# A second sum of squares in SBUF instead of PSUM, and two thirds of the rate for the third pair's input

## The chip, the core and the metric

The kernel runs on one core of a Trainium2 chip. The metric is the device time of one execution, in microseconds. The core has a matrix engine (PE, with its weight load PEld), a vector engine (DVE), a scalar engine (ACT), GpSimd (POOL) and SyncE (SP), which in this kernel issues every DMA in one queue. Matmuls write to PSUM, which the kernel divides into eight banks; everything else is kept in SBUF.

## The reference

One layer of a hybrid encoder: a mixer (retention heads and a convolution module, a joint projection `w_out`) and an MLP, each between two RMSNorms.

```python
mix = jnp.concatenate([ret_out, conv_out.astype(x.dtype)], axis=-1) @ w_out
x = x + rms_norm(mix, g_post_mix)          # first sum of squares: of mix
h = rms_norm(x, g_pre_mlp)                 # second sum of squares: of the new x
f = jnp.square(jax.nn.relu(h @ w_mlp_in)) @ w_mlp_out
x = x + rms_norm(f, g_post_mlp)
```

`d_model` is 1024, the MLP is 4096 wide, and there are 2048 prompt frames, 16 meta tokens and 8 streams of 16 frames. `rms_norm` divides by the root of the mean square over the 1024 channels. All is in fp32; each fp32 product is made of three matmuls of a high and a low part.

## The kernel before, in words

Channels lie on partitions (8 tiles of 128), tokens in the free dimension. The tokens are cut into six blocks (`gi` 0 to 5) of 256 or 384 columns. First the mixer runs over all blocks and leaves the output of `w_out` in DRAM (`yscr`). Then the MLP runs over three pairs of blocks, `G` = 0, 1, 2 (blocks 1 and 2, 3 and 4, 5 and 0), in halves of 384, 384 and 320 columns. For each pair it goes through sixteen blocks `b` of the hidden width. Each `b` has seven products of the first layer (`product`, lines L1207 to L1209, 12 matmuls each; a two by two Strassen scheme), between which lies the second layer of the block before. In `G` = 0, and at the ends of the other pairs, that is plain tiles (`l2_tile`, L514 to L516 through `mm3`, added by L1313). In `G` = 1 and 2, from `b` = 3 to 14, it is fourteen products of a second Strassen scheme (`l2_product`, L1295 to L1297, added to `ya` in SBUF by DVE at L1300). So such a `b` has 21 steps and, after each, a `tick()`.

Weights of the first layer come as prepared products `wp` from DRAM (L296, through SP); those of the second are loaded raw (L338) and prepared on ACT and POOL (L355, L356). Both take turns in one pool of nine buffers, so SP often waits until PE has used one up. L1242 makes differences of three tiles in SBUF on DVE, L383 and L384 split an operand in high and low on ACT and POOL.

Beside the MLP of a pair runs the preparation of the next pair's input: `prologue(G + 1)`, put in the queue "mlp" after `b` = 2. It is a generator; `tick()` advances it by one step when `ticks[0] % slow[0] == 0`, with `slow[0] = 2`. At `b` = 15 `drain("mlp")` would run what is left, and `reload` (L653) then brings the result back to SBUF. The steps are, for each of the two blocks, `mlp_in`:

- first pass: load `yscr` (L549), square on ACT (L501, L504), sum on DVE (L506, L509);
- the sum is copied to SBUF (L571), summed over partitions by a matmul with ones (L473), and eight DVE operations make the reciprocal root in the same PSUM bank, `sw` (L452 to L462), which is read as `rs`;
- second pass: load `yscr` and `x`, scale by `rs` on DVE (L582), add `x` on POOL (L584), store `x1d` (L585), square, and sum again (L506, L509);
- the same copy, matmul and reciprocal root; third pass: load `x1d`, scale (L590), store `hd` (L592).

That is 8 steps in each pass and 2 behind each of the two sums, 28 for a block. Then come `differences` (L614 to L623: loads of `hd`, sixteen subtractions on POOL, stores to `td`), 20 steps, so 76 in all.

The three PSUM pools are `mmp` (3 banks, first layer), `cvp` (2 banks, `l2y` and `mmc`) and `auxp` (3 banks). `auxp` holds `l2w` and `mma` of the second layer, and also the preparation's sum of squares `pacc` and its `sw`. The pool `np_` in SBUF holds `acc` (2 buffers) and `s` (5 buffers). The order of instructions on each engine is not the program's alone: a planner orders them by priority and by its own model of their times, and gives out free buffers as it goes; the preparation has a lower priority (`later["mlp"] = 100`).

Of the kernel before, what the change touches and what calls it, by code (L numbers as in the profile page):

```python
# [12 lines left out]
F32 = mybir.dt.float32  # L13
F32R = mybir.dt.float32r
I32 = mybir.dt.int32
AF = mybir.ActivationFunctionType
# [4 lines left out]
P = 128  # L21
D_MODEL, SEQ, N_META, PAST_LEN = 1024, 2048, 16, 512
# [147 lines left out]
def build(nc, T):  # L170
    lg = _log_gamma()
    with tile.TileContext(nc, schedule_with_timeline_sim=True) as tc, ExitStack() as top:
# [8 lines left out]
        np_ = ep(tc.tile_pool(name="np_", bufs=2))  # L181
# [13 lines left out]
        def pcol(n, i):  # L195
            return par[:, PC[n] + i:PC[n] + i + 1]
# [215 lines left out]

        heads_done = {}

        ticks, slow = [0], [1]

        def tick_heads():
# [29 lines left out]
        def rsqrt(ss, n, y, t, y1, z, r):  # L447


            f = 0.703952253  # L450
            w = 0.375 * f
            nc.vector.tensor_scalar(out=y.bitcast(I32), in0=ss.bitcast(I32), scalar1=-0.5,  # L452
                                    scalar2=float(0x5F1FFFF9) + math.log2(n) * 2.0 ** 22, op0=ALU.mult, op1=ALU.add)
            nc.vector.tensor_tensor(out=t, in0=y, in1=y, op=ALU.mult)
            nc.vector.scalar_tensor_tensor(out=t, in0=t, scalar=-1.0 / n, in1=ss, op0=ALU.mult, op1=ALU.mult)
            nc.vector.scalar_tensor_tensor(out=y1, in0=t, scalar=2.38924456, in1=y, op0=ALU.add, op1=ALU.mult)
            nc.vector.tensor_tensor(out=z, in0=y1, in1=y1, op=ALU.mult)
            nc.vector.scalar_tensor_tensor(out=z, in0=z, scalar=f * f * w ** 0.5 / n, in1=ss, op0=ALU.mult,
                                           op1=ALU.mult)
            nc.vector.scalar_tensor_tensor(out=z, in0=z, scalar=-10.0 / 3.0 * w ** 0.5, in1=z, op0=ALU.add,  # L460
                                           op1=ALU.mult)
            nc.vector.scalar_tensor_tensor(out=r, in0=z, scalar=5.0 * w, in1=y1, op0=ALU.add, op1=ALU.mult)  # L462
            return r
# [4 lines left out]
        def rstd_wide(acc, W, n, out=None):  # L468

            ps = auxp.tile([P, 512], F32, tag="aux", name="sw")[:, :W]  # L470
            accs = acc if isinstance(acc, list) else [acc]
            for i, a in enumerate(accs):
                nc.tensor.matmul(ps, ones, a, start=(i == 0), stop=(i == len(accs) - 1))  # L473
            yield WAIT
            yt = st_tile()
            y, t = yt[:, :W], yt[:, NM:NM + W]
            return rsqrt(ps, n, y, t, y, t, ps if out is None else out)

        def rstd_bcast(acc, W, n):

            starts = list(range(0, W - P + 1, P))
            if starts[-1] + P < W:
                starts.append(W - P)
            nb = len(starts)
            ps = auxp.tile([P, 4, P], F32, tag="aux", name="st")
            for b, s in enumerate(starts):
                nc.tensor.matmul(ps[:, b, :1], acc[:, s:s + P], ones[:, :1], start=True, stop=True)
            y = rsqrt_small(ps[:, :nb, 0], nb, n)
            dg = spool.tile([P, NM // P, P], F32, tag="dg", name="dg", bufs=1)
            for b in range(nb):  # L490
                nc.vector.tensor_scalar(out=dg[:, b, :], in0=ident, scalar1=y[:, b:b + 1], scalar2=None, op0=ALU.mult)
            yield WAIT
            rb = auxp.tile([P, 512], F32, tag="aux", name="rb")
            for b, s in enumerate(starts):
                nc.tensor.matmul(rb[:, s:s + P], ones, dg[:, b, :], start=True, stop=True)
            return rb[:, :W]
# [22 lines left out]
        WM = max(g["W"] for g in LAY)  # L519
# [10 lines left out]
        def st_tile():  # L530
            return stqs[0].tile([P, 2 * NM], F32, tag="st", name="st")

        def s_tile(N):
            return np_.tile([P, WM], F32, tag="s", name="s", bufs=SB)[:, :N]

        def mlp_in(gi):

            g = LAY[gi]
            N, W, m = g["N"], g["W"], g["meta"]
            G, off = PAIR[gi]  # L540
            early = G == 0

            def loads(src, two):

                ahead = []
                for k in range(KT + 1):
                    if k < KT:
                        y = s_tile(N)
                        nc.sync.dma_start(y, src(k))  # L549
                        xk = None  # L550
                        if two:
                            o = g["off"] * KT + k * W + m
                            xk = s_tile(N)
                            nc.sync.dma_start(xk, T["x"][:, o:o + N])
                        ahead.append((k, y, xk))
                    if k:
                        yield ahead.pop(0)

            def summed():
                if early:  # L560
                    return np_.tile([P, WM], F32, tag="acc", name="acc")[:, :N]
                return auxp.tile([P, 512], F32, tag="aux", name="pacc")[:, :N]

            def norm(acc):
                if early:
                    rb = yield from rstd_bcast(acc, N, D_MODEL)
                    rs = tp.tile([P, WM], F32, tag="rs", name="rs", bufs=1)[:, :N]
                    nc.scalar.activation(out=rs, in_=rb, func=AF.Copy)
                    return rs
                sb = np_.tile([P, WM], F32, tag="acc", name="acc")[:, :N]  # L570
                nc.scalar.activation(out=sb, in_=acc, func=AF.Copy)  # L571
                yield WAIT
                return (yield from rstd_wide(sb, N, D_MODEL))

            acc = summed()
            for k, y, _ in loads(lambda k: yscr[gi][k], False):
                add_square(acc, y, k, N)
                yield
            rs = yield from norm(acc)
            acc = summed()  # L580
            for k, y, xk in loads(lambda k: yscr[gi][k], True):
                nc.vector.scalar_tensor_tensor(out=y, in0=y, scalar=pcol("g_post_mix", k), in1=rs, op0=ALU.mult,  # L582
                                               op1=ALU.mult)
                nc.gpsimd.tensor_tensor(out=y, in0=y, in1=xk, op=ALU.add)  # L584
                nc.sync.dma_start(x1d[G][k][:, off:off + N], y)  # L585
                add_square(acc, y, k, N)
                yield
            rs = yield from norm(acc)
            for k, y, _ in loads(lambda k: x1d[G][k][:, off:off + N], False):
                nc.vector.scalar_tensor_tensor(out=y, in0=y, scalar=pcol("g_pre_mlp", k), in1=rs, op0=ALU.mult,  # L590
                                               op1=ALU.mult)
                nc.sync.dma_start(hd[G][k][:, off:off + N], y)  # L592
                yield
# [775 lines left out]
        for G, b, steps in plan():  # L1369
            if b == 0:  # L1370
                drain("norm")
                ya = {(c, r): x1p.tile([P, 4, NM], F32, tag=f"ya{c}{r}", name=f"ya{c}{r}")
                      for c in range(2) for r in range(2)}
            rate["norm"] = 2
            if b == NFB - 1:
                drain("mlp")
            cur, run = layer1(G, b)
            w, ybanks = {}, {}
            for what, x in steps:
                if what == "p":  # L1380
                    next(run)
                    tick()
                elif what == "w":
                    w[x] = next_unit("l2", G, x)
                elif what == "q":
                    wq = next_unit("q", G, x)
                elif what == "u":
                    l2_product(G, b - 1, *x, wq, prev, ya, ybanks)
                    tick()
                else:  # L1390
                    q, o, c = x
                    l2_tile(G, b - 1, c, q, o, w[b - 1, q], prev, ya)
                    tick()
            if b == 2 and G + 1 < NG:
                slow[0] = 2
                queues["mlp"].append(prologue(G + 1))
            if b == NFB - 1:
                if G + 1 < NG:
                    end_layer2(G, b, [w[b, q] for q in range(FB)], cur, ya)
                else:  # L1400
                    last_layer2(G, [w[e, q] for e in (b - 1, b) for q in range(FB)], (prev, cur), ya)
            prev = cur
# [59 lines left out]
```

## Time and profile before

| what | before |
|---|---|
| median of 3 runs | 2396.88 us (2394.41 to 2402.88) |
| the profiled execution | 2391.47 us |
| its span, first to last instruction | 2389.3 us |
| mean granted clock of PE | 0.992 |
| PE busy | 2302.5 us, 96% |
| DVE, POOL, ACT busy | 71%, 63%, 42% |

The mixer takes about the first 945 us of the span. `G` = 0 follows until about 1450, `G` = 1 until about 1950, `G` = 2 until the end. Times of the trace are in us from the start of the span. "Idle before" is the time in which an engine stood still ahead of an instruction, with what released it. A busy PE is not PE at its peak, since its matmuls overlap; where a pace matters, the count of matmuls in a stretch is the better measure.

### The profile page before, as it was taken

To read this page: it belongs to the slowest core of one execution; us is meant where nothing else is said; L and a number is where in the kernel's file an instruction comes from. 1 tells how busy PE (TensorE), PEld (TensorE's weight loads), DVE (VectorE), ACT (ScalarE), POOL (GpSimd) and SP (SyncE) were. 2 spreads that over 40 slices of the span, in tenths; PEclk is the share of its full clock that TensorE was granted. 3 is DMA by queue.
4 is the path that set the end of the run, shared out by engine and by line. 5 is a ranking of instruction groups with operands and counts; after the bars stand their busy time and mean duration, and the time that the engine had idled before them with its cause. 6 is when DMAs were issued, how large, how long until landed. Compare 5 with 4: busy or idle time off the path is not lost. (4 is left out here: it accounts for less than half of the span.)

```text
span 2389.3 us, 41429 instructions
## 1 busy us (share of the span) xinstructions
PE 2302.5 (96%) x14250; PEld 2267.5 (95%) x14250; DVE 1697.1 (71%) x3658; ACT 1002.7 (42%) x2240; POOL 1498.5 (63%) x1562
## 2 busy tenths in 40 slices
PE   8898999999999998999999999999999999999997
PEld 7898999999999998999999999998899999999996
DVE  8999997798988963356643357688776676566666
ACT  5534434124233234444444455344444443544442
POOL 7846232132234136878797775687897747888874
PEclk9999999999999999999999999999999999999998
DMA  8787788898789878568796557666764567555562
GB/s 315 279 314 265 270 294 287 219 336 314 236 292 339 288 268 316 205 215 300 265 329 210 187 203 253 227 222 217 260 220 160 185 221 253 187 193 181 193 218 89
DMA packets 248993, 586.90 MB, mean 246 GB/s; under 512 B 32080, under 2 KB 110160, under 8 KB 248784
## 3 DMA queue, kind: packets, MB, share of 16 engines
q1 hardware_dynamic: 248784, 584.28, 71.9%
q8 instruction: 112, 1.84, 0.3%
q14 instruction: 97, 0.79, 0.1%
HBM read 444.42 MB, written 139.75 MB: 244 GB/s over the span
## 5 line engine op out<-in xcount | busy, mean ns | idle before, releaser
L1207 PE MATMUL mm<-op,wp 128*128 128x384 f32 (+1 forms) x1344 | 443.3, 331 | 14.4 <-DMA wp<-wprod 9.3
L1208 PE MATMUL mm<-op,wp 128*128 128x384 f32 (+1 forms) x1344 | 440.9, 328 | 0.0
L1209 PE MATMUL mm<-op,wp 128*128 128x384 f32 (+1 forms) x1344 | 440.3, 328 | 0.0
L811 DVE SCALAR_TENSOR_TENSOR cv<-ext,par,cv 128x384 f32<-128x384 f32 (+1 forms) x720 | 382.2, 570 | 2.3
L514 PE MATMUL mm<-hhi,whi 128*128 128x384 f32 (+2 forms) x992 | 332.2, 335 | 11.9 <-ACT hhi L707 5.3
L516 PE MATMUL mm<-hhi,wlo 128*128 128x384 f32 (+2 forms) x992 | 329.9, 334 | 10.7 <-POOL wlo L283 4.2
L515 PE MATMUL mm<-hlo,whi 128*128 128x384 f32 (+2 forms) x992 | 331.0, 334 | 0.3
L283 POOL TENSOR_TENSOR wlo<-raw,whi 128x512 fp32r<-128x512 f32 x180 | 238.6, 1345 | 131.0 <-ACT whi L282 54.3
L1300 DVE TENSOR_TENSOR ya<-l2y,ya 128x384 f32<-128x384 f32 (+1 forms) x384 | 194.6, 519 | 115.6 <-PE l2y L1297 114.8
L1207 PEld LDWEIGHTS mm<-op,wp 128*128 128x128 f32 x1344 | 253.9, 189 | 22.9 <-DMA wp<-wprod 9.6
L1208 PEld LDWEIGHTS mm<-op,wp 128*128 128x128 f32 x1344 | 254.1, 189 | 0.1
L1209 PEld LDWEIGHTS mm<-op,wp 128*128 128x128 f32 x1344 | 254.0, 189 | 0.3
L356 POOL TENSOR_TENSOR wq<-raw,wq 128x256 fp32r<-128x256 f32 x240 | 184.0, 780 | 58.8 <-ACT wq L355 56.9
L384 POOL TENSOR_TENSOR fo<-c,fo 128x384 fp32r<-128x384 f32 (+1 forms) x168 | 165.4, 985 | 72.3 <-ACT fo L383 71.2
L514 PEld LDWEIGHTS mm<-hhi,whi 128*128 128x128 f32 x992 | 190.8, 192 | 13.8 <-ACT hhi L707 5.8
L516 PEld LDWEIGHTS mm<-hhi,wlo 128*128 128x128 f32 x992 | 190.2, 192 | 13.6 <-POOL wlo L283 4.8
L515 PEld LDWEIGHTS mm<-hlo,whi 128*128 128x128 f32 x992 | 190.6, 192 | 1.7 <-DVE hlo L708 1.1
L1221 DVE TENSOR_TENSOR c<-mm,sn 128x384 f32<-128x384 f32 (+1 forms) x144 | 76.5, 532 | 127.4 <-PE mm L1209 76.8
L1300 DVE TENSOR_TENSOR ya<-l2w,ya 128x384 f32<-128x384 f32 (+1 forms) x288 | 143.1, 517 | 19.3 <-PE l2w L1297 16.6
L858 POOL TENSOR_TENSOR sw<-sw,sin 128x384 f32<-128x384 f32 (+2 forms) x48 | 48.4, 1009 | 165.2 <-ACT sw L855 161.8
L282 ACT ACTIVATE whi<-raw 128x512 fp32r<-128x512 f32 x192 | 112.6, 623 | 89.6 <-DMA raw<-w_in 20.0
L322 POOL TENSOR_TENSOR wp<-raw,wp 128x512 fp32r<-128x512 f32 x96 | 125.1, 1310 | 37.5 <-ACT wp L321 36.2
(258 smaller groups left out, 6288.8 us busy)
## 6 DMA issues: line engine op xcount, KB each, us to landing
wp<-wprod SPq DMA_DIRECT2D x224, 512.0 KB, 3.9
raw<-w SPq DMA_DIRECT2D x256, 256.0 KB, 3.9
wprod<-wp SPq DMA_DIRECT2D x112, 512.0 KB, 4.2
whi<-wkeep_in SPq DMA_DIRECT2D x108, 512.0 KB, 6.6
wlo<-wkeep_in SPq DMA_DIRECT2D x108, 512.0 KB, 5.9
raw<-w_in SPq DMA_DIRECT2D x72, 256.0 KB, 6.0
whi<-wkeep_out SPq DMA_DIRECT2D x36, 512.0 KB, 6.4
wlo<-wkeep_out SPq DMA_DIRECT2D x36, 512.0 KB, 5.7
```

Of the source, the lines that this page charges most:

```text
L283: (nc.vector if i < 24 and i % 4 == 0 else nc.gpsimd).tensor_tensor(out=lo[:, c], in0=raw, in1=hi[:, c].bitcast(F32), op=ALU.subtract)
L322: tt(out=op[:, H:], in0=src, in1=op[:, :H].bitcast(F32), op=ALU.subtract)
L356: nc.gpsimd.tensor_tensor(out=op[:, o + H:o + 2 * H], in0=src, in1=op[:, o:o + H].bitcast(F32), op=ALU.subtract)
L384: (eng or nc.gpsimd).tensor_tensor(out=lo, in0=src, in1=hi.bitcast(F32), op=ALU.subtract)
L514: nc.tensor.matmul(ps, whi(k), ahi(k), start=(k == 0), stop=False)
L515: nc.tensor.matmul(ps, whi(k), alo(k), start=False, stop=False)
L516: nc.tensor.matmul(ps, wlo(k), ahi(k), start=False, stop=(k == nk - 1))
L811: nc.vector.scalar_tensor_tensor(out=o, in0=src(t), scalar=wt, in1=o, op0=ALU.mult, op1=ALU.add)
L1207: nc.tensor.matmul(ps, hi, ops[:, k, :n], start=start, stop=False, skip_group_check=not first)
L1208: nc.tensor.matmul(ps, hi, ops[:, 4 + k, :n], start=False, stop=False, skip_group_check=not first)
L1209: nc.tensor.matmul(ps, lo, ops[:, k, :n], start=False, stop=(k == 3), skip_group_check=not first)
L1300: last_y[0] = nc.vector.tensor_tensor(out=y, in0=ps, in1=y, op=ALU.add)
```

## The change

The first sum of squares of `mlp_in` stays in a PSUM bank and is copied to SBUF as before. The second is now made in an SBUF tile `acc` from the start when the preparation runs beside the MLP, without a PSUM bank and without the copy; for `G` = 0, which is prepared earlier, both sums were in SBUF before and are so now. And `slow[0]` becomes `2 + G`: the preparation of pair 1 (beside `G` = 0) goes one step every two ticks as before, that of pair 2 (beside `G` = 1) one step every three.

```diff
-            def summed():
-                if early:
+            def summed(beside_norm):
+                if early or beside_norm:
                     return np_.tile([P, WM], F32, tag="acc", name="acc")[:, :N]
                 return auxp.tile([P, 512], F32, tag="aux", name="pacc")[:, :N]
@@
                     return rs
+                yield WAIT
+                return (yield from rstd_wide(acc, N, D_MODEL))
+
+            acc = summed(False)
+            for k, y, _ in loads(lambda k: yscr[gi][k], False):
+                add_square(acc, y, k, N)
+                yield
+            if not early:
                 sb = np_.tile([P, WM], F32, tag="acc", name="acc")[:, :N]
                 nc.scalar.activation(out=sb, in_=acc, func=AF.Copy)
-                yield WAIT
-                return (yield from rstd_wide(sb, N, D_MODEL))
-
-            acc = summed()
-            for k, y, _ in loads(lambda k: yscr[gi][k], False):
-                add_square(acc, y, k, N)
-                yield
+                acc = sb
             rs = yield from norm(acc)
-            acc = summed()
+            acc = summed(True)
@@
             if b == 2 and G + 1 < NG:
-                slow[0] = 2
+                slow[0] = 2 + G
                 queues["mlp"].append(prologue(G + 1))
```

## Rows read from the trace of the kernel before

**Rows 1.** The page, part 1: busy time of each engine.

```profile
PE 2302.5 (96%) x14250; PEld 2267.5 (95%) x14250; DVE 1697.1 (71%) x3658; ACT 1002.7 (42%) x2240; POOL 1498.5 (63%) x1562
```

**Rows 2.** Busy time by stretch; columns: length, engines with counts, clock, DMA.

```profile
1019.00:1260.00 241.00, 236.24 (x1342) 233.63 (x1341) 132.37 (x241) 112.45 (x224) 202.82 (x173) 0.99 0.80 279
1260.00:1400.00 140.00, 140.00 (x810) 140.00 (x808) 49.15 (x90) 58.10 (x110) 106.19 (x88) 1.00 0.55 192
1535.00:1760.00 225.00, 212.22 (x1190) 204.92 (x1189) 187.46 (x340) 104.72 (x254) 190.62 (x232) 1.00 0.72 238
1760.00:1900.00 140.00, 140.00 (x809) 139.76 (x808) 92.98 (x171) 64.60 (x153) 112.00 (x141) 1.00 0.51 167
```

**Rows 3.** Waits of PE, 1535 to 1760 us; columns: total us, times, longest.

```profile
PE mm L1207 <- DMA wp<-wprod: 5.1, 6, 1.9
PE l2w L1295 <- DVE ya L1300: 3.5, 3, 2.0
PE l2y L1295 <- DVE ya L1300: 2.2, 1, 2.2
PE mm L1207 <- ACT fo L383: 1.1, 1, 1.1
PE l2y L1295 <- ACT wq L355: 0.6, 1, 0.6
```

**Rows 4.** Timeline of PE, three stops; columns: start, us, instruction, idle before.

```profile
1163.33 0.44 PE L514 MATMUL mma<-fo,whi 128*128 128x384 f32 x1 [3.49 <-DVE ya L1313]
...
1581.70 0.44 PE L1295 MATMUL l2w<-fo,wq 128*128 128x384 f32 x1 [0.50 <-DVE ya L1300]
...
1741.76 0.44 PE L1295 MATMUL l2y<-fo,wq 128*128 128x384 f32 x1 [2.17 <-DVE ya L1300]
```

**Rows 5.** Timeline of DVE just ahead of the first and third stop.

```profile
1162.19 0.61 DVE L582 SCALAR_TENSOR_TENSOR s<-s,par,sw 128x384 f32<-128x384 f32 x1 [3.24 <-DMA s<-yscr]
...
1735.19 6.05 DVE L1242 TENSOR_TENSOR t<-r,t 128x384 f32<-128x384 f32 x1 [0.63 <-POOL fo L384]
```

**Rows 6.** Timeline of POOL, 1735 to 1741 us, first and last of that stretch.

```profile
1735.75 1.08 POOL L384 TENSOR_TENSOR fo<-c,fo 128x384 fp32r<-128x384 f32 x1
...
1739.91 0.91 POOL L622 TENSOR_TENSOR s<-st 128x320 f32<-128x320 f32 x1
```

**Rows 7.** DVE by line, L509 (1019 to 1760) and L1242 (1535 to 1760): ns min/median/max.

```profile
L509 DVE TENSOR_TENSOR pacc<-pacc,sq x48: 418/555/567, 1020.2 to 1693.9; 128x384 f32<-128x384 f32 x36, 128x256 f32<-128x256 f32 x12
...
L1242 DVE TENSOR_TENSOR c<-c x16: 546/1084/3385, 1537.3 to 1757.0; 128x384 f32<-128x384 f32 x16
L1242 DVE TENSOR_TENSOR t<-c x8: 543/858/1219, 1538.7 to 1756.2; 128x384 f32<-128x384 f32 x8
L1242 DVE TENSOR_TENSOR t<-r,t x7: 541/1141/6048, 1544.2 to 1735.2; 128x384 f32<-128x384 f32 x7
```

**Rows 8.** Waits of SP's queue, 1535 to 1760 us.

```profile
SPq L296 <- PE mm L1209: 42.0, 17, 7.9
SPq L585 <- POOL s L584: 22.9, 11, 4.9
```

**Rows 9.** Waits of SP's queue, 1760 to 1900 us.

```profile
SPq L296 <- PE mm L1209: 48.0, 14, 6.0
SPq L296 <- PE l2y L1297: 42.7, 16, 4.1
```

**Rows 10.** First and last step of the preparation beside G = 1, and the reloads.

```profile
L501 ACT ACTIVATE pacc<-s x4: 368/432/496, 1535.5 to 1673.5; 128x384 f32<-128x384 f32 x2, 128x256 f32<-128x256 f32 x2
...
L623 SPq DMA_DIRECT2D td<-s x16: 319/349/495, 1719.1 to 1755.2; - x16
...
L653 SPq DMA_DIRECT2D st<-td x8: 359/372/768, 1908.0 to 1936.6; - x8
```

**Rows 11.** Busy time by stretch: three second passes (block 4; block 5; block 0).

```profile
1143.00:1181.00 38.00, 34.51 (x191) 34.19 (x190) 19.43 (x37) 18.43 (x39) 32.45 (x29) 0.96 0.77 262
...
1565.00:1604.00 39.00, 36.96 (x209) 35.67 (x208) 33.25 (x61) 22.07 (x53) 36.73 (x44) 1.00 0.75 247
1667.00:1696.00 29.00, 26.91 (x147) 24.72 (x146) 22.01 (x48) 14.20 (x36) 24.97 (x33) 1.00 0.69 217
```

More of the change, by code (lines that the diff above doesn't have):

```diff
@@ L569, in norm @@
                     return rs
-                sb = np_.tile([P, WM], F32, tag="acc", name="acc")[:, :N]
-                nc.scalar.activation(out=sb, in_=acc, func=AF.Copy)
                 yield WAIT
-                return (yield from rstd_wide(sb, N, D_MODEL))
-            acc = summed()
+                return (yield from rstd_wide(acc, N, D_MODEL))
+            acc = summed(False)
             for k, y, _ in loads(lambda k: yscr[gi][k], False):
@@ L578, in mlp_in @@
                 yield
+            if not early:
+                sb = np_.tile([P, WM], F32, tag="acc", name="acc")[:, :N]
+                nc.scalar.activation(out=sb, in_=acc, func=AF.Copy)
+                acc = sb
             rs = yield from norm(acc)
-            acc = summed()
+            acc = summed(True)
             for k, y, xk in loads(lambda k: yscr[gi][k], True):
```

## The prediction, made before the change was run

> **What bounds the kernel now.** I read the shares of the engines first: PE is busy for 2302.5 of 2389.3 us [rows 1], so at most 87 us of standing still can be won in the whole kernel, and only what falls into the two stretches that the change touches counts. So the second view is busy time by stretch [rows 2]: for each pair the stretch in which the next pair's input is prepared, and the quiet one behind it. In both quiet stretches PE never stops and starts a matmul every 0.173 us (140 us by 810, and by 809). Beside the preparation of pair 2 (1535 to 1760 us) it stands still for 225 - 212.2 = 12.8 us; at the quiet pace 225 us would hold 1300 matmuls, and 1190 are there, 19 us short (some records may be missing, and the preparation's own fp32 matmuls are slower, so this is the upper bound of the loss). Beside the preparation of pair 1 (1019 to 1260 us) PE stands still for 4.8 us. No more than about 25 us, 1%, is to be had.
>
> The third view is the waits of PE in the second of these stretches [rows 3]: five groups, twelve stops, 12.5 us of idle time. Two kinds carry it. The first: PE waits for a weight load `wp` that came late (5.1 us, six stops). SP's queue tells why [rows 8, 9]: in the quiet stretch SP waits 90.7 of 140 us for PE to free a buffer, that is, the weights are far ahead; beside the preparation only 42.0 of 225 us go to the largest such wait, while SP stands for 22.9 us behind POOL to store `x1d`, with the next `wp` queued behind. The second kind: PE waits for DVE to empty a bank of the second layer (3.5 and 2.2 us, four stops). The timelines show what held DVE. Ahead of the longest of the four, 2.17 us at 1741.76, [rows 4] a DVE subtraction with both inputs in SBUF took 6.05 us [rows 5] while POOL ran one operation after another [rows 6]. Ahead of the one long stop beside pair 1, 3.49 us at 1163.33, [rows 4] DVE waited 3.24 us for the preparation's own load of `yscr` [rows 5], with the drain of `mma` queued behind it, in a second pass, in which `pacc` and `sw` hold two of the three `auxp` banks.
>
> **The change part by part.** *The PSUM bank.* In a second pass the preparation held two of three `auxp` banks; now it holds one. In the 3.49 us stop PE gets one more tile to work on, six matmuls at 0.173 us, 1.0 us; that stop's second pass also shows a granted clock of 0.96 over 38 us [rows 11], so 1.5 us at half speed went with it (1.2 GHz in place of 2.4); whether a stop of 2.5 us still brings that on no row shows (bounds 0 and 1.5), and I take 0.5. Beside pair 2 one bank wait of 0.50 us, at 1581.70, lies in a second pass [rows 4]; I count it as gone. Together 2.0 us (bounds 0 and 5.5: both stops and the slow clock whole).
>
> *The rate.* The steps are the same 76, at three ticks instead of two: 228 ticks instead of 152. A `b` has 21 ticks and 168 matmuls, 29.1 us at 0.173, so the preparation should take 10.9 `b` and 316 us where it took 7.2 `b` and 211 us and the stops, 220 us in the trace [rows 10]: the two agree, so the planner follows the rate. It ends near 1535 + 316 + 5 = 1856 us. Twelve `b` hold 252 ticks, so it ends 24 ticks (33 us) before `b` = 15, and the reloads of pair 2 at 1908 us [rows 10] stay behind it; the drain at `b` = 15 finds nothing. Nothing is added to any queue; each step's DMAs lie half as far apart again in SP's queue. Late `wp` loads: 5.1 us; the bounds are 0 (the quiet stretch) and 5.1 (each stop belongs to one `x1d` or `hd` store that blocks, however far apart). SP's spare time between two blocks grows, so I take 2.0, a gain of 3.1. Late drains, without the 0.5 above: 3.5 + 2.2 - 0.5 = 5.2 us; bounds 0 and 5.2. DVE is busy for 187.5 of 225 us beside the preparation and 66% in the quiet stretch [rows 2], so the preparation's own share of it is about 187.5 - 149 = 38 us, which over 320 us leaves DVE at 78% in place of 83%: only a little freer. I take 3.0, a gain of 2.2. Waits for `fo` and `wq`, 1.7 us: I take 1.0, a gain of 0.7. A stop also costs the overlap of two matmuls, 0.34 - 0.17 us; with half of twelve stops gone, 1.0. Sum of the rate: 7.0 us (bounds 0 and 14).
>
> *What the SBUF tile costs.* The copy that goes is ACT's, with ACT at 42%: nothing, as ACT's idle time hides it. But 28 DVE additions (seven for each of four blocks) now have both inputs in SBUF, where `pacc` was in PSUM. With PSUM they took 555 ns, at most 567 [rows 7]. The nearest all-SBUF rows, the subtractions of L1242, have medians of 858 to 1141 ns and reach 6048 [rows 7]. So DVE work grows by some 28 x 0.5 = 14 us. Beside pair 1 DVE is idle for half of a second pass (38 us against 19.4) [rows 11] and hides it; beside pair 2 it was idle for 39 - 33.3 and 29 - 22.0 us, which the lower rate lengthens. The price at PE: of the 31 subtractions beside the preparation, I put at most the 5.2 us of late drains to them, 0.17 us each. For the 14 additions beside pair 2 that is 2.4 us; as DVE gets a little freer I take 1.5. Bounds: -0.5 (an add that finds POOL quiet is no slower, and the copy's step falls away) and 28 x 0.55 = 15, when all that the additions grow by reaches PE.
>
> A rule of the Trainium skill speaks against this part. The row shows the flat 567 ns of the PSUM form beside the 6.05 us of the all-SBUF one. The page "SBUF — State Buffer", section "Who interferes with whom", says that a DVE instruction with two SBUF inputs contends with a GpSimd instruction that reads SBUF, through one shared port pair, and that whoever comes second blocks fully; with one SBUF input it does not contend. The trace agrees in both directions of the comparison (567 ns at most, 6048 ns at most). By that rule alone, without a planner that leaves gaps, each of the 28 additions could wait out a POOL operation of 0.9 to 1.3 us; that is the third rival below.
>
> Sum: -2.0 - 7.0 + 1.5 = -7.5 us on the profiled execution, 2391.5 to 2384.0 us. The runs shown have their median 5.4 us above that execution; both should move alike, so the time of the changed kernel is 2396.9 - 7.5 = 2389 us.
>
> **The rivals.** *All stops go.* If the planner needs only these few percent of room, the stretch beside pair 2 runs at the quiet pace: 12.5 + 12 x 0.17 = 14.5 us, with 2 us beside pair 1, 16 in all: 2381 us. For it: the quiet stretches have no stop at all, with DVE at 66%. Against: DVE still has 78% and POOL near 83%.
>
> *The stops only move.* The stores that block SP, the reciprocal roots and the subtractions are all still there, one by one, and the planner makes another order out of them from 1060 us on; where one stop goes another comes. The preparation also keeps one `auxp` bank for half again as long. Then the bounds near 0 hold for the rate, the bank gives 2, the SBUF tile takes 1.5: 2396 us, give or take 4. For it: the stops have their cause in an order, not in a lack of time on any engine. That the change might not do what it says (the rate not followed, or work left for `b` = 15) belongs here; the 24 ticks in hand speak against that.
>
> *Slower: the additions wait for POOL.* The place is the second passes, above all those of blocks 5 and 0, where POOL is busy for 36.7 of 39 and 25.0 of 29 us [rows 11]. If the planner reckons the SBUF form no dearer than the PSUM form, it packs the additions between POOL operations, each takes the 1.1 us and now and then several, and the drains queued behind stop PE. My gains are 9.0, so it breaks even at 9.0 / 28 = 0.32 us of PE for each addition, twice the price seen; at 0.58 us, all that an addition grows by, the kernel is 7.2 us slower, about 2404 us. Against it: the profile shows 0.17 us, and half of the additions lie where DVE is half idle.
>
> **How the numbers follow.** About 0.3%, 7.2 us, is what a measurement of this kernel can tell from no change. My forecast has a chance of 0.50, with 2384 to 2395 us as its own range; as its middle is at that bound, I put 0.28 of it beyond and 0.22 within. All stops go: 0.18, all of it faster. The stops only move: 0.20, all within. The additions wait for POOL: 0.12, slower. That gives 0.46 faster, 0.42 within, 0.12 slower. The range that leaves out 2 in 10 takes the middle of the first rival and most of the third: 2378 to 2402 us.
>
> **What would show it.** In the changed trace the last `td` store should stand near 1855 us, and SP's waits for PE should take a larger share beside the preparation. The waits of PE on `wp` there should fall from 5.1 to about 2 us, those on DVE from 5.7 to about 3, over the longer stretch. No `auxp` bank should be held for the second sum, and the additions of L509 should stand under `acc` with a median near 1 us; if they keep to 0.56 us, the price of the SBUF tile was too high. If PE's waits on DVE grow in the second passes with additions above 2 us ahead of them, the third rival is right; if the waits add up to 12 us again in other places, the second.

## The result and the profile after

| what | before | after |
|---|---|---|
| median of 5 runs | 2398.24 us | 2415.01 us (2406.57 to 2422.10) |
| ratio to before, 95% interval | | 1.0066 (1.0044 to 1.0089) |
| the profiled execution | 2391.47 us | 2415.01 us |
| its span | 2389.3 us | 2413.1 us |

The kernel became slower by 0.66%, 16.8 us at the medians, where 7.5 us of gain were forecast; the time lies beyond the stated range. The two profiled executions are 23.5 us apart; 3.2 us of that lie in the mixer, where the order of instructions on every engine is the same in both (the first matmul of the MLP starts at 935.1 us before and at 938.3 after), so they are spread between executions. Another 6.8 us is what the traced execution before lies under its median; its mean granted clock is 0.992, where 120 executions of that kernel, made beside the experiments, have 0.985 to 0.993 and 0.9892 in the mean. One execution each of `e4_after_shift` (7196 us, the one traced, so that it has no stretches below) and `e10_before_nosub` (10591 us) took several times as long as the others and stands in no median or ratio.

The loss has two places. They are shown here from `b` = 3 to `b` = 15 of each pair, counted from the first matmul of the first layer of the one block to that of the other: busy time by stretch, of the kernel before, then of the kernel after (length, PE, PEld, DVE, ACT and POOL with counts, granted clock, DMA).

```profile
1023.00:1407.60 384.60, 379.83 (x2169) 377.23 (x2169) 180.88 (x329) 170.49 (x333) 310.46 (x261) 1.00 0.71 247
1539.30:1901.40 362.10, 349.32 (x1981) 341.78 (x1980) 277.33 (x505) 166.66 (x399) 299.49 (x369) 1.00 0.64 211
```

```profile
1025.50:1414.50 389.00, 381.22 (x2170) 377.59 (x2169) 194.08 (x329) 170.01 (x331) 317.22 (x261) 0.99 0.71 244
1546.90:1922.70 375.80, 356.12 (x1974) 346.40 (x1973) 276.64 (x503) 165.42 (x397) 304.94 (x369) 0.98 0.62 203
```

Beside the preparation of pair 1 the kernel lost 4.4 us, beside that of pair 2 13.7 us. The work is the same, but for a few records of PE. DVE is busy 13 us longer in the first stretch, with the same 329 instructions, so some of them took longer. The granted clock fell from 1.00 to 0.98 of full in the second: over 376 us that is about 7 us lost, as PE had 1.2 GHz in place of 2.4 for about 14 us behind four of its stops. The other half is waiting: PE's waits after, beside pair 2 (1543 to 1925 us), to be set beside [rows 3].

```profile
PE l2y L1298 <- DVE ya L1303: 10.5, 7, 3.4
PE mm L1210 <- DMA wp<-wprod: 5.6, 6, 1.1
PE l2w L1298 <- DVE ya L1303: 2.3, 2, 1.5
PE mm L1210 <- ACT wq L355: 0.6, 1, 0.6
```

(Line numbers after are up to three higher: L1303 is L1300 of before.) The waits on weights stayed, 5.6 us against 5.1. The waits on DVE went from 5.7 us to 12.8. That is 6.5 us more of waiting in all, and with the slow clock it makes the 13.7 us.

That holds for these two traces. The mean granted clock of all five executions after is 0.9886, against the 0.9892 of before; a thousandth of it is 2.4 us, so of the 16.8 us at the medians the clock accounts for an estimated 1 to 2. And two traces of one order differ: `e6_mixphase` below, with DVE's order of before beside pair 2, took 366.9 us, and a second trace of the kernel after 371.5, so that the two orders lie 9 us apart in the mean, 364.5 and 373.7.

What held DVE is seen in its timeline. Beside pair 1 it is one of the new additions, `acc<-acc,sq`; beside pair 2 the longest is the old subtraction `t<-r,t`. First DVE, two stretches of the kernel after, then POOL in the same two stretches.

```profile
1169.48 6.75 DVE L510 TENSOR_TENSOR acc<-acc,sq 128x384 f32<-128x384 f32 x1 [1.64 <-ACT sq L505]
1176.88 0.56 DVE L510 TENSOR_TENSOR acc<-acc,sq 128x384 f32<-128x384 f32 x1 [0.65 <-ACT sq L505]
1177.36 0.55 DVE L1316 TENSOR_TENSOR ya<-mmc,ya 128x384 f32<-128x384 f32 x1
...
1807.16 8.40 DVE L1245 TENSOR_TENSOR t<-r,t 128x384 f32<-128x384 f32 x1 [0.53 <-POOL fo L384]
1815.49 0.54 DVE L1303 TENSOR_TENSOR ya<-l2y,ya 128x384 f32<-128x384 f32 x1
```

```profile
1168.85 1.02 POOL L587 TENSOR_TENSOR s<-s 128x384 f32<-128x384 f32 x1
1169.83 1.29 POOL L312 TENSOR_TENSOR s<-raw 128x512 f32<-128x512 f32 x1
1171.08 1.31 POOL L322 TENSOR_TENSOR wp<-raw,wp 128x512 fp32r<-128x512 f32 x1
1172.34 1.03 POOL L384 TENSOR_TENSOR fo<-c,fo 128x384 fp32r<-128x384 f32 x1
1173.31 1.29 POOL L313 TENSOR_TENSOR raw<-raw 128x512 f32<-128x512 f32 x1
1174.54 1.28 POOL L322 TENSOR_TENSOR wp<-raw,wp 128x512 fp32r<-128x512 f32 x1
...
1807.76 0.91 POOL L625 TENSOR_TENSOR s<-st,s 128x320 f32<-128x320 f32 x1
1808.60 0.90 POOL L625 TENSOR_TENSOR s<-st 128x320 f32<-128x320 f32 x1
1809.44 1.46 POOL L356 TENSOR_TENSOR wq<-raw,wq 128x256 fp32r<-128x256 f32 x2
1810.84 1.04 POOL L384 TENSOR_TENSOR fo<-c,fo 128x384 fp32r<-128x384 f32 x1
1811.81 0.76 POOL L349 TENSOR_TENSOR raw<-raw,raw 128x256 f32<-128x256 f32 x1
1812.51 0.88 POOL L625 TENSOR_TENSOR s<-st,s 128x320 f32<-128x320 f32 x1
1813.32 0.88 POOL L625 TENSOR_TENSOR s<-st 128x320 f32<-128x320 f32 x1
1814.14 1.02 POOL L384 TENSOR_TENSOR fo<-r,fo 128x384 fp32r<-128x384 f32 x1
```

In both places POOL starts one operation as the one before ends, and the DVE operation, both of whose inputs lie in SBUF, ends only when that row of POOL operations does: at 1176.2, after POOL's last end at 1175.8, and at 1815.6, after 1815.2. Most such operations do not fare so: of 52 in this trace (1019 to 1950 us) that started with 3 us or more of such a row ahead, four waited it out and the others took at most 1.72 us. The drains of PSUM banks queue behind it, and PE stops. PE in those two stretches:

```profile
1173.46 0.34 PE L1211 MATMUL mm<-op,wp 128*128 128x384 f32 x1
1177.96 0.69 PE L515 MATMUL mmc<-fo,whi 128*128 128x384 f32 x1 [4.17 <-DVE ya L1316]
...
1812.37 0.34 PE L1212 MATMUL mm<-op,wp 128*128 128x384 f32 x1
1816.09 0.44 PE L1298 MATMUL l2y<-fo,wq 128*128 128x384 f32 x1 [3.38 <-DVE ya L1303]
```

### The profile page after: what moved, and what is told of

Same layout as the page of the kernel before. It is cut to its first block, busy times and chain, and to the rows that moved or that the text cites. A ratio compares the mean times of both kernels' runs of the same rounds, so it can differ in the third digit from the quotient of the medians.

```text
span 2413.1 us, 41398 instructions
## 1 busy us (share of the span) xinstructions
PE 2313.0 (96%) x14250; PEld 2274.3 (94%) x14250; DVE 1713.2 (71%) x3658; ACT 1000.4 (41%) x2236; POOL 1511.8 (63%) x1562
## 4 chain that ended last, share of the span: by engine, by line
PE 65%; DVE 13%; DMA 12%; POOL 5%; issue 4%; ACT 1%; SPq 1%; DVEq 0%; POOLq 0%; ACTq 0%
PE mm L1210 7%; PE mm L1212 7%; PE mm L1211 7%; PE mm L517 6%; PE mm L516 6%; PE mm L515 6%; DMA wp<-wprod 2%; DMA s<-yscr 2%; PE mma L515 2%; PE mmc L515 2%; PE mma L516 2%; PE mma L517 2%; PE mmc L517 2%; PE mmc L516 2%; DVE cv L814 2%
## 5 line engine op out<-in xcount | busy, mean ns | idle before, releaser
L1303 DVE TENSOR_TENSOR ya<-l2y,ya 128x384 f32<-128x384 f32 (+1 forms) x384 | 194.2, 519 | 124.4 <-PE l2y L1300 123.2
L1303 DVE TENSOR_TENSOR ya<-l2w,ya 128x384 f32<-128x384 f32 (+1 forms) x288 | 141.3, 516 | 13.1 <-PE l2w L1300 11.1
```

Source lines behind the costliest of these rows:

```text
L1303: last_y[0] = nc.vector.tensor_tensor(out=y, in0=ps, in1=y, op=ALU.add)
```

## The experiments

They were made to tell apart three theories: A, the additions in SBUF are the loss; B, the lower rate is; C, neither has a price of its own, but the planner makes another order, and each order has its own stops. Later ones ask what in an order is dear (D). Times are medians; every ratio is to the kernel before on the same chip.

**The SBUF sum alone** (`e1_sbuf`), against the kernel after:

```diff
-                slow[0] = 2 + G
+                slow[0] = 2
```

> The SBUF sum alone: pair 2 is prepared at the old rate, one step in two ticks. Theory A (the additions that wait for POOL are the loss): the whole loss of the changed kernel is here, 2411 to 2416 us against 2398, with a stop of 4 us behind a long addition beside G = 0. Theory B (the lower rate is the loss): G = 1 costs nothing, only G = 0 keeps its 4 us: 2400 to 2404 us. Theory C (the order that the planner makes anew is the loss, and neither part has a price of its own): G = 0 as in the changed kernel, 4 us, since its order is the same; G = 1 moves by some us up or down, not predictable, anywhere from 2394 to 2414.

Measured: 2402.80 us, ratio 1.0004 (0.9988 to 1.0021). Beside pair 1 the trace has 388.7 us from `b` = 3 to 15 and the same long addition (6.7 us), beside pair 2 366.5 us. Theory A falls: the loss isn't here alone.

**The lower rate alone** (`e2_rate`), against the kernel before:

```diff
-                slow[0] = 2
+                slow[0] = 2 + G
```

> The lower rate alone: one step in three ticks beside G = 1, both sums in PSUM as before. The order up to G = 1 is that of the kernel before. Theory A: no loss, or the 7 us of gain that was forecast for the rate: 2390 to 2398 us. Theory B: the 14 us that G = 1 lost in the changed kernel: about 2412 us. Theory C: anything between, and the two parts alone don't add up to the change.

Measured: 2401.85 us, ratio 1.0017 (0.9999 to 1.0035); 365.3 us beside pair 2. Theory B falls, and so does the gain that was forecast for the rate: it is no gain and at most a small loss. The two parts alone come to 1.0021 together, and the change to 1.0066.

**The same work, one tick later.** `e3_shift` moves every step of the preparation of the kernel before by one tick, `e4_after_shift` those of the kernel after, `e5_after_shift2` by two:

```diff
-            if ticks[0] % slow[0] == 0:
+            if (ticks[0] + 1) % slow[0] == 0:
```

> The kernel before with every step of the preparation one tick later: the same instructions, banks, buffers and rate, only the planner's starting point differs. Theories A and B: nothing that they name has changed, so within 0.3% of before, 2391 to 2405 us, with stops beside the preparation of about 17 us in all as before. Theory C: the order differs, and the stops beside G = 0 and G = 1 add up to another sum, 6 us or more away from before in one direction or the other.

Measured: 2399.68 us, ratio 1.0000 (0.9987 to 1.0012). The time stayed, but not the stretches: 380.6 us beside pair 1 (384.6 before) and 372.0 beside pair 2 (362.1). Their sum in this one trace is 5.9 us longer, about the 6 us that C expected, but the time over twelve executions doesn't show it. So the order alone, with no change of work, rate or banks, moves a stretch by up to 10 us, of which up to 5 us are what two traces of one order differ by.

> The changed kernel with every step of the preparation one tick later. Theories A and B: as the changed kernel, 2409 to 2422 us. Theory C: another order, another sum of stops: 6 us or more away from the changed kernel, perhaps under the kernel before.

Measured: 2405.59 us, ratio 1.0033 (1.0011 to 1.0054): half the loss.

> The changed kernel with every step of the preparation two ticks later, the third of the three places that a step in three ticks can take beside G = 1 (beside G = 0, where a step comes every two ticks, the order is the changed kernel's own). Theory C (the time of a stretch belongs to the order that the planner makes): G = 0 stays at 201 to 202 us from b = 3 to 9, as in the changed kernel; G = 1 is another draw, between 362 and 376 us from b = 3 to 15, so 2399 to 2415 us. Theory A or B (the two parts have a fixed price): 2411 to 2416 us, with 375 us in that stretch.

Measured: 2408.55 us, ratio 1.0041 (1.0023 to 1.0059); 384.3 us beside pair 1, 374.2 beside pair 2. The first number tells most. The order beside pair 1 is the same as in the kernel after, but in this execution no addition waited out a row of POOL operations. The additions by line, of the kernel after and of this one (1019 to 1260 us; ns min/median/max):

```profile
L510 DVE TENSOR_TENSOR acc<-acc,sq x12: 548/789/6752, 1076.8 to 1182.1; 128x384 f32<-128x384 f32 x12
```

```profile
L510 DVE TENSOR_TENSOR acc<-acc,sq x12: 643/926/1437, 1072.1 to 1174.9; 128x384 f32<-128x384 f32 x12
```

With the same order, and a longer median, the stretch is 4.7 us shorter, as long as before (384.6): what the SBUF sum costs beside pair 1 hangs on that one addition and the slow clock behind its stop (some 2 us lost in the kernel after, none here).

The row of POOL operations was there too. Here are the same addition, the next one, and POOL beside them:

```profile
1164.65 0.80 DVE L510 TENSOR_TENSOR acc<-acc,sq 128x384 f32<-128x384 f32 x1 [2.12 <-ACT sq L505]
1166.10 0.92 DVE L510 TENSOR_TENSOR acc<-acc,sq 128x384 f32<-128x384 f32 x1 [0.65 <-ACT sq L505]
```

```profile
1163.04 2.00 POOL L587 TENSOR_TENSOR s<-s 128x384 f32<-128x384 f32 x2
1164.98 1.63 POOL L312 TENSOR_TENSOR s<-raw 128x512 f32<-128x512 f32 x1
1166.57 1.63 POOL L322 TENSOR_TENSOR wp<-raw,wp 128x512 fp32r<-128x512 f32 x1
```

In both executions the addition starts 0.63 to 0.65 us into the second L587, with the same POOL operations behind it. Here it got its turn in 0.80 us, and POOL's L312 took 1.63 us in place of 1.29; there it waited for the whole row. So a row without a gap doesn't settle it, and what does is not shown.

**A second trace of the kernel after** (`e8_after_again`), without an edit:

> The changed kernel once more, for a second trace of the same order. Theory C: the stretches repeat to about 2 us, 202 us beside G = 0 from b = 3 to 9 and 375 us beside G = 1 from b = 3 to 15, with the same long DVE operations in the same places; only the mixer ahead of them moves by some us. If the loss were chance of one execution, the stretch beside G = 1 would come back nearer to the 362 us of before.

Measured: 2411.58 us in one run; 388.2 us beside pair 1 and 371.5 beside pair 2, with a 6.7 us addition and a 7.7 us `t<-r,t` in the same places. The loss repeats, to some 4 us.

**One tick later beside pair 1 alone** (`e6_mixphase`), against the kernel before:

```diff
-            if ticks[0] % slow[0] == 0:
+            if (ticks[0] + phase[0]) % slow[0] == 0:
@@
-                slow[0] = 2
+                slow[0], phase[0] = 2, 1 - G
```

> The kernel before, with the steps one tick later beside G = 0 alone; beside G = 1 the order is again that of the kernel before. Theory C: G = 0 takes from the shifted kernel its 189 us from b = 3 to 9 (197 before), G = 1 keeps the 362 us of before from b = 3 to 15, so the kernel is 8 us faster than before: 2390 to 2393 us, ratio 0.996 to 0.998. Theories A and B: nothing that they name has changed, ratio 1.000.

Measured: 2392.61 us, ratio 0.9981 (0.9962 to 1.0000). DVE's order beside pair 2 is again that of before; the stretches are 382.9 and 366.9 us. The 8 us were taken from too short a stretch (up to `b` = 9; 4 of them came back by `b` = 15). It is the fastest of the variants that do the whole work, but hardly told from before. The two stops of 2.0 and 2.2 us beside pair 2 in [rows 3] are there again, with 2.29 and 2.17 us, and this time the clock fell behind each of them: 3.4 us lost, which before had not.

**The freed bank held all the same** (`e7_hold`), against the SBUF sum alone:

```diff
             acc = summed(True)
+            bank = None if early else auxp.tile([P, 512], F32, tag="aux", name="pacc")[:, :N]
@@
                 add_square(acc, y, k, N)
+                if k == 0 and not early:
+                    nc.scalar.activation(out=bank, in_=y, func=AF.Copy)
                 yield
+            if not early:
+                nc.scalar.activation(out=bank, in_=bank, func=AF.Copy)
```

> The SBUF sum alone (old rate), with the PSUM bank that it frees held all the same through the second pass: ACT copies one tile into the bank at its start, and the bank onto itself at its end. If the freed bank is worth something and the additions in SBUF cost something, this keeps the cost and gives up the gain: 2 to 6 us above the SBUF sum alone, 2405 to 2409 us. Theory C: again another order and another draw, from 2392 to 2412 us, so that the two are not told apart by it.

Measured: 2402.15 us, ratio 1.0016 (1.0000 to 1.0032); 386.5 and 364.1 us. The order is another one from the first second pass on, and the ratio can't be told from that of the SBUF sum alone. What the bank is worth stays open: the two ratios differ by 3 us, and each is known to 4.

**Each part one tick later.** `e11_rate_shift` and `e12_sbuf_shift` are the lower rate and the SBUF sum, each alone, with the edit of `e3_shift`.

> The lower rate alone with every step one tick later. If the rate has a price of its own, the ratio is that of the rate alone, 1.0017, within 0.15%; if each order is a draw, it may lie between 0.998 and 1.006. With the two parts together three orders gave 1.0066, 1.0033 and 1.0041.

Measured: 2399.07 us, ratio 1.0003 (0.9986 to 1.0021); 382.4 and 363.4 us.

> The SBUF sum alone with every step one tick later. If the SBUF sum has a price of its own, 1.0004 within 0.15%; if each order is a draw, between 0.996 and 1.006, with the G = 0 stretch from b = 3 to 15 anywhere from 380 to 390 us according to whether an addition waits for POOL for several us (6.7 us of one addition gave 388 to 389 us, none above 1.5 us gave 384 us).

Measured: 2403.56 us, ratio 1.0029 (1.0010 to 1.0048); 383.5 us beside pair 1, where no addition took above 1.6 us, and 372.7 us beside pair 2, with a `t<-r,t` of 8.3 us. So the SBUF sum alone gives 1.0004 in one order and 1.0029 in another, and in the second the stretch that grew holds a long operation that it does not touch. At this offset the two parts add up to the whole: 1.0003 and 1.0029 make 1.0032, and `e4_after_shift` has 1.0033; at the first offset they don't (1.0021 and 1.0066).

**Without POOL's subtractions in the differences** (`e9_after_nosub` from the kernel after, `e10_before_nosub` from that before):

```diff
-                    t = s_tile(n)
-                    nc.gpsimd.tensor_tensor(out=t, in0=x, in1=y, op=ALU.subtract)
-                    nc.sync.dma_start(td[G][i, k], t)
-                    ts.append(t)
+                    nc.sync.dma_start(td[G][i, k], x)
+                    ts.append(x)
```

> The changed kernel without the sixteen subtractions that POOL makes in the differences of each later pair (left out: one term of each difference, so pairs 1 and 2 get other operands; the loads and stores stay). Theory D: beside G = 1 the loss is a long DVE subtraction that cannot read while POOL runs one operation after another, and the differences, thinned to one in three ticks, fill POOL's last gaps just where such subtractions stand. Then the 8 us t<-r,t goes, PE's waits on DVE fall from 12 to 6 us or less and the stretch of G = 1 from b = 3 to 15 from 372 to 376 us to about 362 us; the kernel is at 2397 to 2401 us. Theory E (the loss is the freed bank, the SBUF sums or the loads that SP issues): the stretch stays above 370 us and the kernel at 2408 us or more.

Measured: 2402.58 us, ratio 1.0011 (0.9991 to 1.0031). The 8 us `t<-r,t` is gone, the stretch beside pair 2 is 365.1 us, and PE's waits on DVE there are 7.7 us (1543 to 1920 us; L1296 and L1301 are the L1295 and L1300 of before):

```profile
PE l2y L1296 <- DVE ya L1301: 6.2, 4, 2.6
PE mm L1208 <- DMA wp<-wprod: 5.7, 7, 2.6
PE l2w L1296 <- DVE ya L1301: 1.5, 1, 1.5
```

> The kernel before without the same sixteen subtractions. Theory D: it gains less than the changed kernel does, as its stops have more kinds of cause (5.1 us on weights, 5.7 us on DVE): G = 1 from b = 3 to 15 goes from 362 to 367 us to about 358 us, the kernel to 2393 to 2396 us, 3 to 6 us under the changed kernel without them (where 14 us part the two with them). Theory E: both gain the same, and 14 us still part them.

Measured: 2392.37 us, ratio 0.9978 (0.9958 to 0.9997); 360.2 us beside pair 2. With POOL's sixteen subtractions gone from both, the ratios lie 8 us apart, give or take 7, where 16 parted the two kernels. That agrees with D for about half of the loss, more roughly than it said (3 to 6 us, waits of 6 us or less and a stretch of 362 us were expected), and it can't rule out the 14 us of E. Beside pair 1 the 6.7 us addition, and 388.6 us, remained.

**That DVE subtraction on POOL** (`e13_after_pool` from the kernel after, `e14_before_pool` from that before), which keeps all work:

```diff
-            def diff(out, a, b):
-                nc.vector.tensor_tensor(out=out, in0=a, in1=b, op=ALU.subtract)
+            def diff(out, a, b, eng=None):
+                (eng or nc.vector).tensor_tensor(out=out, in0=a, in1=b, op=ALU.subtract)
@@
-                    operand(P4, diff(t2, b21, t2))
+                    operand(P4, diff(t2, b21, t2, nc.gpsimd))
```

> The changed kernel with the last subtraction of each block of the second scheme, t<-r,t, made by POOL instead of DVE (24 operations of 0.5 to 8.4 us on DVE become 24 of about 1 us on POOL). If this DVE operation, held up while POOL runs one operation after another, is what makes the stretch beside G = 1 slow, the stretch falls from 372 to 376 us to 362 to 366 us and the kernel to 2402 to 2406 us (ratio 1.002 to 1.003: the 4 us beside G = 0 stay). If long operations were only a sign of a lack of time on POOL, the stretch stays above 370 us, as POOL gets 24 us more work, and the ratio at 1.005 or more.

Measured: 2409.85 us, ratio 1.0034 (1.0016 to 1.0052). The stretch beside pair 2 fell to 368.6 us and half of the loss went, which is less than expected, and no more than a new offset alone gave (1.0033 and 1.0041). PE's waits on DVE were still 11.1 us, in nine pieces of 2.1 us at most; of the 7.3 us by which the stretch is shorter, 5 are less slow clock.

> The kernel before with the same subtraction on POOL. It had one such operation of 6.0 us, with a stop of 2.2 us behind it. If the mechanism is right, up to 3 us faster, 2395 to 2399 us, ratio 0.998 to 1.000; if POOL's extra time counts more, slower by some us, ratio 1.001 to 1.004.

Measured: 2408.48 us, ratio 1.0032 (1.0018 to 1.0047); 372.2 us beside pair 2: the second of the two outcomes, and the trace shows a place. `t<-r,t` no longer waits, but POOL, which now makes it too, had a long row without a gap, and another DVE operation with both inputs in SBUF, the square in the reciprocal root, waited it out; PE stopped for 6.5 us behind it. The same edit goes with a lower ratio in the kernel after and a higher one in the kernel before. DVE in that stretch, and the first and last POOL operation that it waited out:

```profile
1608.24 9.84 DVE L454 TENSOR_TENSOR st<-st 128x384 f32<-128x384 f32 x1
1618.00 0.55 DVE L1300 TENSOR_TENSOR ya<-l2w,ya 128x384 f32<-128x384 f32 x1
```

```profile
1608.84 0.73 POOL L349 TENSOR_TENSOR raw<-raw,raw 128x256 f32<-128x256 f32 x1
...
1616.93 0.73 POOL L348 TENSOR_TENSOR s<-raw,raw 128x256 f32<-128x256 f32 x1
```

All traces but that of `e4_after_shift`, ordered by the stretch beside pair 2 (us from `b` = 3 to 15 of each pair; the longest DVE operation with both inputs in SBUF in each):

| kernel | pair 1: stretch | longest | pair 2: stretch | longest | ratio |
|---|---|---|---|---|---|
| `e10_before_nosub` | 387.3 | 1.7 | 360.2 | 3.5 | 0.9978 |
| before | 384.6 | 3.4 | 362.1 | 6.0 | 1 |
| `e11_rate_shift` | 382.4 | 2.0 | 363.4 | 5.9 | 1.0003 |
| `e7_hold` | 386.5 | 1.7 | 364.1 | 1.4 | 1.0016 |
| `e9_after_nosub` | 388.6 | 6.7 | 365.1 | 3.8 | 1.0011 |
| `e2_rate` | 385.5 | 1.5 | 365.3 | 6.0 | 1.0017 |
| `e1_sbuf` | 388.7 | 6.7 | 366.5 | 1.4 | 1.0004 |
| `e6_mixphase` | 382.9 | 2.0 | 366.9 | 6.1 | 0.9981 |
| `e13_after_pool` | 388.2 | 6.7 | 368.6 | 4.4 | 1.0034 |
| `e8_after_again` | 388.2 | 6.7 | 371.5 | 7.7 | |
| `e3_shift` | 380.6 | 2.0 | 372.0 | 8.3 | 1.0000 |
| `e14_before_pool` | 386.0 | 1.5 | 372.2 | 9.8 | 1.0032 |
| `e12_sbuf_shift` | 383.5 | 1.6 | 372.7 | 8.3 | 1.0029 |
| `e5_after_shift2` | 384.3 | 1.6 | 374.2 | 8.4 | 1.0041 |
| after | 389.0 | 6.8 | 375.9 | 8.4 | 1.0066 |

Beside pair 2, every trace with such an operation of 7.7 us or more has 371.5 to 375.9 us (six traces), and every other 360.2 to 368.6 (nine). Beside pair 1, every trace with the 6.7 us addition has 388.2 to 389.0 us (five), and every other 380.6 to 387.3 (ten). The kernel after has both. Below that the length orders nothing: 6 us goes with 362 to 367 us, 1.4 us with 364 to 367. The limit was read from these same traces, and most orders have one trace. The timelines show that a long operation makes a stop of PE, 3.38 us behind the one of 8.40. That it makes most of the difference beside pair 2 is argued: `e9` and `e13` are without it and have shorter stretches, but both also have another order and less slow clock, and the waits on DVE of `e13` fell by 1.7 us only.

## Why the prediction was wrong

**What bounds the kernel**: right. PE's stops beside the preparation are where most of the change is, and the quiet stretch behind that of pair 1 runs without a stop after the change too (140 us by 809 matmuls). Behind that of pair 2 it doesn't: PE is busy for 77.7 of 80 us (1824 to 1904 us).

**The sum's largest term, the rate: wrong in both parts, and the step that failed was to price the stops by the load of an engine.** For late drains 2.2 us of gain were taken, as DVE would be "a little freer". In the two traces they grew by 7.1 us, from 5.7 to 12.8. The bounds given, 0 and 5.2, had no room for growth: I had excluded a loss because no work was added. But the longest of these stops come from DVE operations that waited out a row of POOL operations, and these come and go with the order, and from one execution to the next. For late weights 3.1 us of gain were taken; they stayed, 5.6 us against 5.1. SP hardly had more time: it waited for PE to free a buffer for 92.0 of 281 us in the three rows below, 33%, and before for 63.3 of 225 us, 28% (the 42.0 of [rows 8] and the three rows of before here). The rate alone, at 1.0017 and 1.0003, gave 1 to 4 us of loss at the middle of its intervals where 7.0 us of gain were put. SP's queue beside pair 2 after (1543 to 1824 us), then before (1535 to 1760 us):

```profile
SPq L296 <- PE mm L1212: 52.9, 19, 7.9
SPq L296 <- PE l2y L1300: 31.9, 14, 5.1
...
SPq L296 <- PE l2w L1300: 7.2, 4, 3.4
```

```profile
SPq L296 <- PE l2w L1296: 12.3, 5, 4.1
...
SPq L296 <- PE l2w L1297: 6.1, 7, 2.9
...
SPq L296 <- PE l2y L1297: 2.9, 5, 2.0
```

**That the planner follows the rate: wrong for the part that mattered.** 316 us were worked out for the preparation, and it took 276 (1543.0 to 1819.5 us). Its last part, the differences, should take 20 steps of three ticks, 83 us. Their stores after:

```profile
L626 SPq DMA_DIRECT2D td<-s x16: 319/320/485, 1783.4 to 1819.5; - x16
```

They span 36.1 us, as in [rows 10], where they span 36.1 us too though two ticks for each of 20 steps would make 55. The rate thinned the passes; POOL's sixteen subtractions came as densely as before, and the 8.4 us subtraction on DVE stands among them. I had the number for before in [rows 10] and did not work it out: only the sum over the whole preparation was compared.

**The SBUF sum: the mechanism was right, its place was not.** DVE's additions do wait for POOL. Of its price little can be said: +1.5 us was put, and the SBUF sum alone, with the bank that it frees, came to 1 us and 7 us in two orders. I put the price on pair 2, as DVE is half idle beside pair 1. Beside pair 2 the twelve `acc` additions of L510 had a median of 576 ns and at most 1235; beside pair 1 one took 6752 ns, and that cost a stop of 4.2 us and some slow clock. As the stop of 3.5 us that before had is gone, the rest of PE's longer waits there (7.7 us against 4.8) is two waits for `fo`, 3.3 us against 0.7. Idle time of DVE hides a slow operation only if nothing is queued behind it; here the drains were. The long wait came with DVE half idle, so DVE's load did not decide it. The rule that was weighed ("SBUF — State Buffer" of the Trainium skill, section "Who interferes with whom") has its direction confirmed, with one difference: from a lock that is held for one instruction I had worked out a wait of one POOL operation, 0.9 to 1.3 us. In the fifteen traces (1019 to 1950 us) 752 DVE additions, subtractions and products of two SBUF tiles started with 2.5 us or more of a gapless POOL row ahead: 712 were done within 1.74 us, as that working had it, and 40 waited for the whole row. The rows above show such waits for five operations and for more, 6.75 and 8.40 us, and the measurement decides.

**The PSUM bank**: about 2 us of gain were taken; nothing in the runs shows it. The 3.49 us stop beside pair 1 went, and one of 4.17 us came.

**The rivals.** The third (the additions wait for POOL) names the mechanism, but in blocks 5 and 0, where it did not come. The second (the stops only move) describes best what happened, and its time, 2396 us give or take 4, was too kind: it let stops move but not grow. The slow clock that follows a stop wasn't in its price, nor in mine for pair 2; it is half of the loss there in these two traces, but 1 to 2 us at the medians. Chances of 0.12 for slower and a range up to 2402 us followed from bounds that let nothing grow.

**What stays open**: why all three orders with both parts lost (1.0066, 1.0033, 1.0041) while each part alone lost from nothing to 1.0029. The traces of two of these orders both have an operation of 8 us beside pair 2; three orders are too few to say that both parts together must lead there. Nor is it shown that the parts have no fixed price: at one offset they add up. What decides whether a DVE operation gets its turn between two POOL operations is open, and of the 16.8 us at the medians the part that lies outside these waits isn't placed.

## What to carry to other kernels

A change that gives the planner other work makes a new order, and where stops come from meetings of two engines that come and go with the order, as here, the new order is close to a draw: measure the same change at a second offset, and trace an order twice, before its parts are given a price. Ahead of that, list the operations of one engine that can be held by a row of another's, with their longest time and what is queued behind them; that list says more of what can be lost than the share of busy time. And compare the planner's pace step by step, not over the whole, before counting on a rate.

## What the runs showed of the hardware

A DVE operation with both inputs in SBUF that starts in a row of POOL operations without a gap did one of two things. Mostly it got its turn: 712 of 752 were done within 1.74 us, and POOL's operation beside it could take longer, 1.63 us in place of 1.29. Or it got none until the row ended, and finished 0.3 to 0.4 us after it: 6.75, 8.40 and 9.84 us were measured where 0.55 us is the time without POOL. The same addition, at the same place in the same row, did the one in one execution and the other in another.

The granted clock fell to 1.2 GHz for some us after some of PE's stops and not after others. Three waits of 1.9 to 2.2 us beside pair 2 before had none [rows 3]; two of them, at 2.29 and 2.17 us in `e6_mixphase`, had one, and so had a wait of 2.02 us after. Four such falls cost 6.8 us, 1.7 each, as much as a short stop itself (1.49 us ahead of the last of them).
